# HGRN levels scored in pairs, state updates and scores in fewer runs, and the running maximum spread through DRAM, in a decoder layer on one core

## The chip, the cores and the metric

The kernel runs on one core of one Trainium2 chip. The metric is the device time of one execution in microseconds (us); the median of the runs shown is given. TensorE does the matmuls, VectorE (DVE), ScalarE (ACT) and GpSimd (POOL) the elementwise work, SyncE (SP) starts most DMAs.

## What is computed

One layer on x of 512 tokens by 1024 channels, all in float32:

```python
x = x + 0.5 * rms_norm(swiglu_ffn(rms_norm(x, pre0), ffn1_in, ffn1_out), post0)
x = x + rms_norm(token_mixer(rms_norm(x, pre1)), post1)
x = x + 0.5 * rms_norm(swiglu_ffn(rms_norm(x, pre2), ffn2_in, ffn2_out), post2)
```

The token mixer projects its input by one matrix of 4104 columns and feeds two causal mixers of four heads each. HGRN2 is a gated linear recurrence, S_t = diag(f_t) S_{t-1} + k_t v_t^T and o_t = S_t^T q_t. The mLSTM also keeps a matrix state C, and it scales its scores by exp(a_s - M_t), where M is a running maximum over the tokens, one row per head. The outputs of both are normalised, gated and projected back.

## The kernel before, in words

**Dense work.** Every large product is made of float32r matmuls in three parts, high by high, high by low and low by high (`mm3`, L124-128, and `in_k`, L429-433). Weights come by DMA from SP into a ring (`load`, L183), ACT rounds the high part (L208), DVE takes the low part (L210).

**The mixer stage** (L1388) has two kinds of TensorE work. The column groups of the projection are jobs, written as generators: `job_f` (L746) yields 8 times with 6 matmuls of 256 columns each, `job_t` (L762) yields 32 times with 3 matmuls of 512 columns each. `fill(n)` (L732) takes n such steps from the queue of jobs, and `until(name)` (L741) takes steps until a job is done. Between the fills stand the small float32 matmuls of the mixers, written out by hand in the order in which TensorE does them. A planner puts the instructions of each engine in order ahead of time, by when it expects them to be ready; on the chip each engine keeps that order.

**HGRN.** Inside a chunk of 128 tokens the scores are made by levels of block sizes 64, 32, 16, 8, 4 and 2 (`LEVELS`), for two heads at a time (pass 0 and pass 1). A level (`hgrn_level`, L1038) has four steps: two DVE subtractions and two ACT exponentials (L1050 to L1053); a DVE product (L1055); 32 or 64 recorded small matmuls that use 32 columns of the array (L1068), 640 of them in all; and `put`, which places the scores. `hgrn_levels` (L1073) prepares level n+1, fills 7 steps (pass 0) or 5 (pass 1), and then scores level n. The tag `st` has four buffers, and the levels share them with the convolution and the mLSTM; the two `ke` tiles are taken in turn. `hgrn_states` (L1099) computes the states after chunks 0, 1 and 2 with two fill steps behind each.

**mLSTM.** `gate_rows` (L1150) makes the four rows of -M as a float32r pair `nm` (L1170, L1171). `neg_m` (L1190) spreads a row over the 128 partitions with a matmul by a selector `sel` (L1193), which `masks` builds on POOL (L912 to L922). It is called six times: once per head for the gains e (L1217 to L1221) and once per pair of heads for the decays (L1266 to L1277). The scores (L1231) use 64 rows of the array, the keys are transposed (L1283), and the updates of the state C (L1297) use 64 of its columns, in three runs with two fill steps behind each.

**Gain rows.** The tiles `gpre` and `gpost` hold a norm's gain on all partitions. `gain` (L97, DMA at L99) loads them on SP's queue; `mix_out0` asks for `gpost` and the third norm for `gpre`, both after the mixers.

Of the kernel before, what the change touches and what calls it, by code (L numbers as in the profile page):

```python
# [26 lines left out]
FILL = (7, 5, 2, 2)  # L27
# [40 lines left out]
class Layer:  # L68
    def __init__(self, ctx, tc, aps):
        self.tc, self.nc = tc, tc.nc  # L70
        self.__dict__.update(aps)
        nc = self.nc
        pool = lambda name, **kw: ctx.enter_context(tc.tile_pool(name=name, bufs=1, **kw))
        self.cp, self.wp, self.sp, self.psp = pool("cp"), pool("wp"), pool("sp"), pool("psp", space=PSUM)
        self.uid, self.hold = 0, ()
        self.wt, self.free, self.slot = None, deque(range(WBUF)), {}

        self.ident = self.cp.tile([P, P], F32, name="ident")
        make_identity(nc, self.ident)
# [7 lines left out]
    def nm(self, s):  # L87
# [3 lines left out]
    def ps(self):  # L91
        return self.psp.tile([P, 512], F32, tag="ps", bufs=8, name=self.nm("ps"))

    def col(self, n=1):
        return self.sp.tile([P, n], F32, tag=f"col{n}", bufs={1: 12}.get(n, 4), name=self.nm("col"))

    def gain(self, tag, row):  # L97
        g = self.cp.tile([P, D], F32, tag=tag, bufs=1, name=self.nm(tag))
# [3 lines left out]
    def gain_pe(self, tag, row):  # L102

        nc = self.nc
        g = self.cp.tile([P, D], F32, tag=tag, bufs=1, name=self.nm(tag))
# [58 lines left out]
    def load_due(self, n):  # L164
        lds = self.due.pop(n, ())
        for ld in lds:
            pool = self.wp if ld.ring == "raw" else self.hpool
            self.raw[ld.key] = pool.tile([P, ld.a, ld.b], F32, tag=ld.ring, bufs=ld.depth, name=self.nm(ld.ring))
# [173 lines left out]
    def junk(self):  # L342
        return self.sp.tile([P, 512], F32, tag="junk", bufs=1, name=self.nm("junk"))
# [17 lines left out]
    def pre(self, i, g):  # L361
# [6 lines left out]
        else:  # L368
            xn = self.sp.tile([P, D], F32, tag="xn", bufs=1, name=self.nm("xn"))
# [86 lines left out]
    def open_ffn(self, ctx):  # L456

        hp = self.hpool = ctx.enter_context(self.tc.tile_pool(name=self.nm("hp"), bufs=1))
        self.hf = hp.tile([P, NF, T], F32, name=self.nm("hf"))
        self.xf = [self.hf[:, j : j + 2, :].rearrange("p a (b t) -> p (a b) t", t=HALF) for j in (NF - 4, NF - 2)]  # L460
        sq = [hp.tile([P, 2 * D + PAD], F32R, tag="s", bufs=3, name=self.nm("sq")) for _ in range(3)]
# [203 lines left out]
    def h_tile(self, k2, dst=None):  # L665

        t = dst
        if t is None:
            t = self.place(self.hpool.tile([P, 2 * D + PAD], F32R, tag="s", bufs=3, name=self.nm("hs")), 2)
# [213 lines left out]
    def masks(self, mc, mb):  # L883
# [27 lines left out]
        sel = mb.tile([4, 6, 2, 64], F32, tag="tmp", bufs=1, name="sel")  # L911
        nc.gpsimd.memset(sel, 1.0)  # L912
        self.sel = mc.tile([36, 6, P], F32R, name="selr")
        nc.gpsimd.memset(self.sel.bitcast(I32), 0)
        for n in range(6):
            pat = [[0, 2], [0, 64]] if n < 4 else [[-1, 2], [0, 64]]
            base = -n if n < 4 else -2 * (n - 4)
            nc.gpsimd.affine_select(
                sel[:, n], sel[:, n], pattern=pat, compare_op=ALU.is_equal, fill=0.0, base=base, channel_multiplier=1
            )  # L920
        for r in (0, 32):
            nc.gpsimd.tensor_copy(self.sel[r : r + 4], sel.rearrange("p n a b -> p n (a b)"))  # L922
    def forget_gates(self, mb):
# [4 lines left out]
        for p in range(2):  # L928
            f = (self.sp, mb)[p].tile([P, 2, T], F32, tag=("xn", "tmp")[p], bufs=1, name=self.nm("f"))
# [8 lines left out]
        for p, f in enumerate(fs):  # L938
# [5 lines left out]
            kk = mb.tile([P, 2, T], F32, tag="kk", bufs=2, name=self.nm("kk"))  # L944
# [4 lines left out]
        for p, f in enumerate(fs):  # L949
            G = mb.tile([P, 2, T], F32, tag="G", bufs=2, name=self.nm("G"))  # L950
# [7 lines left out]
    def st(self, name, n=512, dt=F32):  # L958
        return self.sp.tile([P, n], dt, tag="st", bufs=4, name=self.nm(name))

    def hgrn_decays(self, p):
# [14 lines left out]
        d = self.sp.tile([P, 2, T], F32, tag="xn", bufs=1, name=self.nm("ek"))  # L976
# [15 lines left out]
    def hgrn_lowest(self, p):  # L992
# [5 lines left out]
        one = self.sp.tile([P, 2, T], F32, tag="xn", bufs=1, name=self.nm("one"))  # L998
# [74 lines left out]
    def hgrn_levels(self, p, kes, per, then=lambda: None):  # L1073
# [4 lines left out]
        self.fill(per // 2)  # L1078
        next(L[0])
        d = self.hgrn_decays(p)  # L1080
        self.fill(per // 2)
        next(L[1])
        next(L[0])
        self.fill(per)
        for n in range(1, N):
            if n == 2:
                self.hgrn_edges(p, d)
                then()
            if n + 1 < N:
                next(L[n + 1])  # L1090
            next(L[n])
            if n > 1:
                next(L[n - 1])
            self.fill(per)
            next(L[n])
        next(L[N - 1])
        self.spread(p)

    def hgrn_states(self):  # L1099

        nc = self.nc
        for c in range(NT - 1):
            ps = self.ps()
            for h in range(NH):
                nc.tensor.matmul(
                    ps[:, h * P : (h + 1) * P], self.kdt[:, h, c * P : (c + 1) * P], self.vh[:, c, h, :], start=True, stop=True
                )
            if c == 0:
# [7 lines left out]
            self.fill(2)  # L1116
# [33 lines left out]
    def gate_rows(self, mc):  # L1150
# [17 lines left out]
        nm = mc.tile([36, T], F32R, name="nm2")  # L1168
        nc.gpsimd.memset(nm.bitcast(I32), 0)
        nc.vector.tensor_scalar(nm[0:4], M, -1.0, None, op0=ALU.mult)  # L1170
        nc.vector.scalar_tensor_tensor(nm[32:36], M, -1.0, nm[0:4].bitcast(F32), op0=ALU.mult, op1=ALU.subtract)  # L1171
        self.nm2 = nm
# [17 lines left out]
    def neg_m(self, n):  # L1190
        ps = self.ps()
        mm = self.nc.tensor.matmul
        mm(ps, self.sel[:, n, :], self.nm2, start=True, stop=True)  # L1193
        return ps

# [12 lines left out]
    def mlstm_pair(self, p):  # L1208

        nc = self.nc  # L1210
        es = []
        for h in (2 * p, 2 * p + 1):
            nm = self.neg_m(h)
            nm4 = nm.rearrange("p (c t) -> p c t", c=NT)
            e = self.st("e")
            e4 = e.rearrange("p (c t) -> p c t", c=NT)
            nc.vector.tensor_tensor(e4, nm4, self.aT[:, :, h : h + 1].broadcast_to([P, NT, P]), op=ALU.add)  # L1217
            nc.vector.tensor_copy(self.nend[:, h, :].rearrange("p (c o) -> p c o", o=1), nm4[:, :, P - 1 : P])
            nc.vector.tensor_scalar(e, e, 0.0, None, op0=ALU.min)
            nc.scalar.activation(e, e, AF.Exp)  # L1220
            nc.gpsimd.affine_select(  # L1221
                e4, e4, pattern=[[0, NT], [1, P]], compare_op=ALU.is_ge, fill=0.0, base=0, channel_multiplier=-1
            )
            es.append(e)
            yield
        scs = [self.ps(), self.ps()]
        for c in range(NT):
            s = slice(c * P, (c + 1) * P)
            for a in range(2):
                o = slice(64 * a, 64 * a + 64)  # L1230
                nc.tensor.matmul(scs[a][:, s], self.qk[o, 2 + p, s], self.qk[o, p, s], start=True, stop=True)  # L1231
        yield
        for a in range(2):
            nc.vector.scalar_tensor_tensor(self.pT[:, 2 * p + a, :], scs[a], 0.125, es[a], op0=ALU.mult, op1=ALU.mult)
        yield

    def mlstm_scores(self, mc):

        nc = self.nc
        self.nend = mc.tile([P, NH, NT], F32, name="nend")  # L1240
        self.pT = mc.tile([P, NH, T], F32, name="pT")
        H = [self.mlstm_pair(p) for p in range(2)]
        next(H[0])
        next(H[0])
        self.fill(3)
        next(H[1])
        self.fill(3)
        next(H[0])
        next(H[0])
        next(H[1])  # L1250
        self.fill(6)
        next(H[1])
        next(H[1])
        w = mc.tile([P, NT, NH], F32, name="w")
        nc.vector.tensor_tensor(w, self.aT, self.nend.rearrange("p h c -> p c h"), op=ALU.add)
        nc.scalar.activation(w, w, AF.Exp)
        self.qdm = mc.tile([P, 2, 3 * P], F32, name="qdm")
        self.kw = mc.tile([P, 2, 3, P], F32, name="kw")

        self.C = mc.tile([P, 2, 3, 258], F32, name="C")  # L1260
        nc.gpsimd.memset(self.C, 0.0)
        dcs = []
        for p in range(2):
            nm = self.neg_m(4 + p)
            ns = self.st("ns")
            nc.scalar.copy(ns, nm)  # L1266
            n4 = ns.rearrange("p (c t) -> p c t", c=NT)
            d = self.st("dq", 3 * P)
            nc.vector.tensor_tensor(
                d.rearrange("p (c t) -> p c t", c=3), n4[:, 1:, :], n4[:, :3, P - 1 : P].broadcast_to([P, 3, P]), op=ALU.subtract  # L1270
            )
            nc.scalar.activation(d, d, AF.Exp)
            dc = self.col(2)
            nc.vector.tensor_tensor(
                dc.rearrange("p (c o) -> p c o", o=1), n4[:, 1:3, P - 1 : P], n4[:, 0:2, P - 1 : P], op=ALU.subtract
            )
            nc.scalar.activation(dc, dc, AF.Exp)  # L1277
            dcs.append(dc)
            wp = self.col(8)[:, :6]
            nc.vector.tensor_copy(wp.rearrange("p (c a) -> p c a", a=2), w[:, :3, 2 * p : 2 * p + 2])  # L1280
            pt = self.ps()
            for c in range(3):
                nc.tensor.transpose(pt[:, c * P : (c + 1) * P], self.qk[:, 2 + p, c * P : (c + 1) * P], self.ident)  # L1283
            nc.vector.tensor_tensor(
# [6 lines left out]
            self.fill(3)  # L1291
        for c in range(3):
            for p in range(2):
                ps = self.ps()
                for a in range(2):
                    r, v = slice(64 * a, 64 * a + 64), slice(129 * a, 129 * a + 129)
                    nc.tensor.matmul(  # L1297
# [272 lines left out]
```

## Time and profile before

| | before |
|---|---|
| median of 3 runs | 943.44 us (942.9 to 943.52) |
| profiled execution | 943.6 us, of which the span is 941.9 us |
| TensorE (PE) busy | 933.0 us |
| VectorE / ScalarE / GpSimd busy | 701.1 / 470.0 / 291.1 us |
| granted TensorE clock | 0.999 |

The span runs from the first to the last instruction of the profiled execution; 1.7 us of its time lie around it. PE is the row of matmuls, PEld that of the weight loads ahead of them. Matmuls overlap in the records, so what one costs is read from start to start. A row of the timeline gives start, duration, engine, line, operation, tiles, shape and how many records it merges; a float32 matmul leaves two records. A row of a group gives busy time and the mean of one in ns, then the idle time before it.

### The profile page before, as it was taken

What the parts mean: (1) busy time and instruction counts of PE and PEld (TensorE: products, weight loads), DVE (VectorE), ACT (ScalarE), POOL (GpSimd) and SP (SyncE); (2) the same over time, 40 slices, a digit from 0 to 9 for tenths busy, and PEclk for the clock granted to TensorE, in tenths of its full rate; (3) what the DMA queues carried; (4) which work ended last, traced back from release to release, by engine and by line L of the source; (5) the groups of instructions that cost most, each with busy time, mean ns of one, the idle gap of its engine ahead of it and who ended that gap; (6) DMA issues with size and microseconds to landing.
All of it is one profiled execution on the core that took longest, in us unless ns stands there. A gap on an engine that the chain in (4) does not pass through costs nothing.

```text
span 941.9 us, 16851 instructions
## 1 busy us (share of the span) xinstructions
PE 933.0 (99%) x7027; PEld 851.7 (90%) x7027; DVE 701.1 (74%) x788; ACT 470.0 (50%) x641; POOL 291.1 (31%) x234
## 2 busy tenths in 40 slices
PE   9999999999999999999999999999999999999997
PEld 7999999999888889998777888999999999988885
DVE  6798999998545466798746665887999999844543
ACT  7645444445434345987634254753544444533431
POOL 3545555661000037200011301354555655100001
PEclk9999999999999999999999999999999999999999
DMA  9243333425332006331222126204324332332202
GB/s 319 85 135 113 112 110 118 133 90 162 106 104 98 0 23 167 104 91 54 83 69 68 45 76 216 90 26 133 113 90 135 119 106 91 112 106 96 90 0 90
DMA packets 81671, 96.05 MB, mean 102 GB/s; under 512 B 4117, under 2 KB 61497, under 8 KB 81594
## 3 DMA queue, kind: packets, MB, share of 16 engines
q1 hardware_dynamic: 81306, 94.44, 31.3%
q8 instruction: 55, 0.90, 0.4%
q10 hardware_dynamic: 288, 0.52, 0.2%
q14 instruction: 22, 0.18, 0.1%
HBM read 92.85 MB, written 2.10 MB: 101 GB/s over the span
## 4 chain that ended last, share of the span: by engine, by line
PE 92%; DVE 3%; POOL 2%; issue 1%; ACT 1%; DVEq 0%; POOLq 0%; ACTq 0%
PE ps L488 46%; PE ps L126 12%; PE ps L128 12%; PE ps L127 12%; PE ps L433 6%; PE ps L267 1%; PE ps L1068 1%; POOL col L259 1%; POOL col L354 0%; DVE w L216 0%; PE ps L1138 0%; PE ps L115 0%; PE ps L122 0%; DVE y L1330 0%; ACT junk L353 0%
## 5 line engine op out<-in xcount | busy, mean ns | idle before, releaser
L210 DVE TENSOR_TENSOR w<-raw,w 128x1024 fp32r<-128x1024 f32 x214 | 363.0, 1703 | 124.9 <-ACT w L208 124.5
L208 ACT CAST w<-raw 128x1024 fp32r<-128x1024 f32 x214 | 224.0, 1052 | 297.4 <-PE ps L128 96.5
L222 POOL TENSOR_TENSOR raw<-raw,raw 128x1024 f32<-128x1024 f32 x80 | 221.0, 2764 | 171.9 <-DVE w L210 161.4
L488 PE MATMUL ps<-xq,w 128*128 128x256 f32 x2016 | 238.1, 277 | 0.0
L488 PEld LDWEIGHTS ps<-xq,w 128*128 128x128 f32 x2016 | 233.7, 188 | 0.2
L488 PE MATMUL ps<-sq,w 128*128 128x256 f32 x1440 | 171.0, 277 | 0.0
L488 PEld LDWEIGHTS ps<-sq,w 128*128 128x128 f32 x1440 | 167.4, 188 | 0.0
L128 PE MATMUL ps<-w,hs 128*128 128x512 f32 x336 | 131.0, 390 | 0.0
L126 PE MATMUL ps<-w,hs 128*128 128x512 f32 x336 | 130.9, 390 | 0.0
L127 PE MATMUL ps<-w,hs 128*128 128x512 f32 x336 | 130.8, 389 | 0.0
L126 PE MATMUL ps<-w,xq 128*128 128x512 f32 x208 | 84.6, 407 | 0.4 <-DVE y L1371 0.3
L128 PE MATMUL ps<-w,xq 128*128 128x512 f32 x208 | 81.2, 392 | 0.3 <-DVE xq L274 0.3
L127 PE MATMUL ps<-w,xq 128*128 128x512 f32 x208 | 81.3, 392 | 0.0
L128 PEld LDWEIGHTS ps<-w,hs 128*128 128x128 f32 x336 | 63.1, 188 | 13.8 <-DVE hs L672 0.7
L126 PEld LDWEIGHTS ps<-w,hs 128*128 128x128 f32 x336 | 63.1, 188 | 12.9
L127 PEld LDWEIGHTS ps<-w,hs 128*128 128x128 f32 x336 | 63.1, 188 | 12.7
L354 POOL TENSOR_SCALAR col<-col 128x1 f32<-128x1 f32 x24 | 9.6, 398 | 199.3 <-ACT junk L353 199.1
L433 PE MATMUL ps<-xq,w 128*128 128x256 f32 x480 | 55.8, 278 | 0.0
L433 PEld LDWEIGHTS ps<-xq,w 128*128 128x128 f32 x480 | 55.2, 188 | 0.2 <-issue 0.2
L672 DVE TENSOR_TENSOR hs<-hf,hs 128x1024 fp32r<-128x1024 f32 x42 | 51.1, 1217 | 0.0
L126 PEld LDWEIGHTS ps<-w,xq 128*128 128x128 f32 x208 | 39.1, 188 | 10.2 <-issue 1.6
L128 PEld LDWEIGHTS ps<-w,xq 128*128 128x128 f32 x208 | 39.1, 188 | 9.3 <-DVE xq L274 0.8
(235 smaller groups left out, 922.7 us busy)
## 6 DMA issues: line engine op xcount, KB each, us to landing
raw<-in_ffn_w_in_dram SPq DMA_DIRECT2D x88, 512.0 KB, 4.4
raw<-in_ffn_w_out_dram SPq DMA_DIRECT2D x44, 512.0 KB, 3.6
raw<-in_w_mix_in_dram SPq DMA_DIRECT2D x28, 512.0 KB, 3.7
raw<-in_w_mix_out_dram SPq DMA_DIRECT2D x8, 512.0 KB, 3.7
out_dram<-xs SPq DMA_DIRECT2D x8, 256.0 KB, 2.0
xs<-in_x_dram SPq DMA_DIRECT2D x6, 256.0 KB, 6.4
gpost<-in_norm_post_dram SPq DMA_DIRECT2D x3, 512.0 KB
gpre<-in_norm_pre_dram SPq DMA_DIRECT2D x2, 512.0 KB, 4.1
```

The source lines that it names most:

```text
L126: mm(ps, sh, mh, start=start, stop=False, **kw)
L127: mm(ps, sh, ml, start=False, stop=False, **kw)
L128: mm(ps, sl, mh, start=False, stop=stop, **kw)
L208: nc.scalar.copy(hi, raw)
L210: nc.vector.tensor_tensor(lo, raw, hi.bitcast(F32), op=ALU.subtract)
L222: nc.gpsimd.tensor_tensor(o, o, c, op=ALU.add)
L259: nc.gpsimd.tensor_tensor(r, m, self.nhalf[:, :n], op=ALU.pow)
L267: self.nc.tensor.transpose(pt[:, c * P : (c + 1) * P], src[:, k * P : (k + 1) * P], self.ident)
L354: nc.gpsimd.tensor_scalar(m, ss, s2 / D, b, op0=ALU.mult, op1=ALU.add)
L433: mm(ps[:, u0:u1], w[:, a, k, :], self.xop(k, b, u0, u1), start=k + n + m == 0, stop=k == ND - 1 and n == 2, skip_group_check=True,)
L488: self.nc.tensor.matmul(ps[:, c], wb[b][:, k, v], left[d][:, k, :], start=first and a + n + k == 0, stop=n == 2 and k == KH - 1, skip_grou ...
L672: self.nc.vector.tensor_tensor(t[:, 1], src, t[:, 0].bitcast(F32), op=ALU.subtract)
```

## The change

- `hgrn_levels` takes the levels two by two: the small matmuls of levels (1, 2), (3, 4) and (5, 6) stand together, with 15 fill steps ahead of each pair in pass 0 and 12 in pass 1. The next pair is prepared when the last one has been scored.
- `hgrn_states` takes a list: chunks 0 and 1 stand together, and chunk 2 stands ahead of the updates of C. Those are one run; C has 129 columns instead of 258 and its DVE updates take all 128 partitions at once.
- `neg_m`, its selector and its six matmuls go. The rows -M are written to DRAM and read back on all 128 partitions, by three DMAs on POOL's queue, into the tiles `gpre` and `gpost`.
- The gains of all four heads come first; then, for each pair of heads, the decays, the scores and the transposes stand together with 8 fill steps behind them.
- HGRN's values are made two chunks at a time.

The diff, cut to its core (`nm` is renamed `name` everywhere):

```diff
-FILL = (7, 5, 2, 2)
+FILL = (15, 12, 2, 2)
...
+        self.dp = pool("dp", space=bass.MemoryType.DRAM)
...
         next(L[0])
-        self.fill(per // 2)
+        self.fill(3)
         next(L[0])
         d = self.hgrn_decays(p)
-        self.fill(per // 2)
-        next(L[1])
+        self.fill(3)
+        both = lambda n: [next(L[m]) for m in (n, n + 1)]
+        both(1)
         next(L[0])
-        self.fill(per)
-        for n in range(1, N):
-            if n == 2:
+        for n in range(1, N, 2):
+            both(n)
+            if n > 1:
+                both(n - 2)
+            self.fill(per)
+            both(n)
+            if n == 1:
                 self.hgrn_edges(p, d)
                 then()
-            if n + 1 < N:
-                next(L[n + 1])
-            next(L[n])
-            if n > 1:
-                next(L[n - 1])
-            self.fill(per)
-            next(L[n])
-        next(L[N - 1])
+            if n + 2 < N:
+                both(n + 2)
+        both(N - 2)
         self.spread(p)
...
-    def hgrn_states(self):
+    def hgrn_states(self, chunks):
...
-            self.fill(2)
...
-        nm = mc.tile([36, T], F32R, name="nm2")
...
+        nm = mc.tile([4, T], F32, name="nm2")
+        nc.vector.tensor_scalar(nm, M, -1.0, None, op0=ALU.mult)
+        rows = self.dp.tile([4, T], F32, name="mrows")
+        nc.gpsimd.dma_start(rows, nm)
+        self.nm = []
+        for p, tag in enumerate(("gpre", "gpost")):
+            t = self.cp.tile([P, D], F32, tag=tag, bufs=1, name=self.name(tag)).rearrange("p (a t) -> p a t", a=2)
+            nc.gpsimd.dma_start(t, rows[2 * p : 2 * p + 2].rearrange("(o a) t -> o a t", o=1).broadcast_to([P, 2, T]))
+            self.nm += [t[:, 0], t[:, 1]]
...
-    def neg_m(self, n):
-        ps = self.ps()
-        mm = self.nc.tensor.matmul
-        mm(ps, self.sel[:, n, :], self.nm2, start=True, stop=True)
-        return ps
...
+    def mlstm_gains(self, h):
...
+        nc.vector.tensor_tensor(
+            e4, self.nm[h].rearrange("p (c t) -> p c t", c=NT), self.aT[:, :, h : h + 1].broadcast_to([P, NT, P]), op=ALU.add
+        )
+        nc.vector.tensor_scalar(e, e, 0.0, None, op0=ALU.min)
+        nc.scalar.activation(e, e, AF.Exp)
+        nc.gpsimd.affine_select(
+            e4, e4, pattern=[[0, NT], [1, P]], compare_op=ALU.is_ge, fill=0.0, base=0, channel_multiplier=-1
+        )
+        return e
...
+        es = [self.mlstm_gains(h) for h in range(NH)]
+        self.fill(3)
         dcs = []
         for p in range(2):
...
+            for a in range(2):
+                r = slice(64 * a, 64 * a + 64)
+                n4 = self.nm[2 * p + a][r].rearrange("p (c t) -> p c t", c=NT)
+                nc.vector.tensor_tensor(
+                    d[r].rearrange("p (c t) -> p c t", c=3), n4[:, 1:, :], n4[:, :3, P - 1 : P].broadcast_to([64, 3, P]), op=ALU.subtract
+                )
...
+            self.fill(8)
+        self.hgrn_states((2,))
+        banks = [self.ps(), self.ps()]
+        for p in range(2):
+            for c in range(3):
                 for a in range(2):
                     r = slice(64 * a, 64 * a + 64)
...
+                    nc.tensor.matmul(
+                        banks[p][r, 129 * c : 129 * c + 129], self.kw[:, p, c, r], self.vm[:, c, 2 * p + a, :],
+                        start=True, stop=True, skip_group_check=True,
+                    )
...
+        self.fill(4)
...
-                self.hgrn_states()
+                self.hgrn_states((0, 1))
+                self.fill(6)
                 self.mlstm_scores(mc)
...
-                self.chunks(self.hgrn_values, FILL[3])
+                for pair in ((0, 1), (2, 3)):
+                    G = [self.hgrn_values(c) for c in pair]
+                    for _ in range(2):
+                        for g in G:
+                            next(g)
+                        self.fill(2)
+                    self.fill(2)
+                    for g in G:
+                        next(g)
```

More of the change, by code (lines that the diff above doesn't have):

```diff
@@ L456, in open_ffn @@
     def open_ffn(self, ctx):
-        hp = self.hpool = ctx.enter_context(self.tc.tile_pool(name=self.nm("hp"), bufs=1))
-        self.hf = hp.tile([P, NF, T], F32, name=self.nm("hf"))
+        hp = self.hpool = ctx.enter_context(self.tc.tile_pool(name=self.name("hp"), bufs=1))
+        self.hf = hp.tile([P, NF, T], F32, name=self.name("hf"))
         self.xf = [self.hf[:, j : j + 2, :].rearrange("p a (b t) -> p (a b) t", t=HALF) for j in (NF - 4, NF - 2)]
-        sq = [hp.tile([P, 2 * D + PAD], F32R, tag="s", bufs=3, name=self.nm("sq")) for _ in range(3)]
+        sq = [hp.tile([P, 2 * D + PAD], F32R, tag="s", bufs=3, name=self.name("sq")) for _ in range(3)]
         self.sq = [self.place(t, KH, True) for t in sq]
@@ L668, in h_tile @@
         if t is None:
-            t = self.place(self.hpool.tile([P, 2 * D + PAD], F32R, tag="s", bufs=3, name=self.nm("hs")), 2)
+            t = self.place(self.hpool.tile([P, 2 * D + PAD], F32R, tag="s", bufs=3, name=self.name("hs")), 2)
         src = self.hf[:, 2 * k2 : 2 * k2 + 2, :]
@@ L910, in masks @@
             nc.gpsimd.tensor_copy(self.eye[r], square[r, r])
[L911 to L922, printed above, removed]
     def forget_gates(self, mb):
@@ L997, in hgrn_lowest @@
         by2 = lambda t: flat(t).rearrange("p (b two) -> p b two", two=2)
-        one = self.sp.tile([P, 2, T], F32, tag="xn", bufs=1, name=self.nm("one"))
+        one = self.sp.tile([P, 2, T], F32, tag="xn", bufs=1, name=self.name("one"))
         near = self.st("near")
@@ L1107, in hgrn_states @@
                 )
+            banks.append(ps)
+        for c, ps in zip(chunks, banks):
             if c == 0:
@@ L1206, in conv @@
             nc.vector.scalar_tensor_tensor(y[:, s:], x[:, : T - s], tap(j), y[:, s:], op0=ALU.mult, op1=ALU.add)
-    def mlstm_pair(self, p):
+    def mlstm_gains(self, h):
         nc = self.nc
[L1211 to L1235, printed above, removed]
@@ L1237, in mlstm_scores @@
+        return e
     def mlstm_scores(self, mc):
         nc = self.nc
-        self.nend = mc.tile([P, NH, NT], F32, name="nend")
-        self.pT = mc.tile([P, NH, T], F32, name="pT")
[L1242 to L1254, printed above, removed]
@@ L1255, in mlstm_scores @@
-        nc.vector.tensor_tensor(w, self.aT, self.nend.rearrange("p h c -> p c h"), op=ALU.add)
-        nc.scalar.activation(w, w, AF.Exp)
+        nend = mc.tile([P, NH, NT], F32, name="nend")
+        for h in range(NH):
+            nc.vector.tensor_copy(
+                nend[:, h, :].rearrange("p (c o) -> p c o", o=1), self.nm[h].rearrange("p (c t) -> p c t", c=NT)[:, :, P - 1 : P]
+            )
+        self.pT = mc.tile([P, NH, T], F32, name="pT")
         self.qdm = mc.tile([P, 2, 3 * P], F32, name="qdm")
@@ L1258, in mlstm_scores @@
         self.kw = mc.tile([P, 2, 3, P], F32, name="kw")
-        self.C = mc.tile([P, 2, 3, 258], F32, name="C")
-        nc.gpsimd.memset(self.C, 0.0)
+        self.C = mc.tile([P, 2, 3, 129], F32, name="C")
+        w = mc.tile([P, NT, NH], F32, name="w")
+        nc.vector.tensor_tensor(w, self.aT, nend.rearrange("p h c -> p c h"), op=ALU.add)
+        nc.scalar.activation(w, w, AF.Exp)
+        es = [self.mlstm_gains(h) for h in range(NH)]
+        self.fill(3)
         dcs = []
         for p in range(2):
[L1264 to L1271, printed above, removed]
+            d = mc.tile([P, 3 * P], F32, tag="dq", bufs=2, name=self.name("dq"))
+            dc = self.col(2)
+            for a in range(2):
[4 more added lines that the diff above has]
+                )
+                nc.vector.tensor_tensor(
+                    dc[r].rearrange("p (c o) -> p c o", o=1), n4[:, 1:3, P - 1 : P], n4[:, 0:2, P - 1 : P], op=ALU.subtract
+                )
@@ L1281, in mlstm_scores @@
+            for c in range(NT):
+                s = slice(c * P, (c + 1) * P)
+                for a in range(2):
+                    o = slice(64 * a, 64 * a + 64)
+                    nc.tensor.matmul(scs[a][:, s], self.qk[o, 2 + p, s], self.qk[o, p, s], start=True, stop=True)
             pt = self.ps()
@@ L1283, in mlstm_scores @@
                 nc.tensor.transpose(pt[:, c * P : (c + 1) * P], self.qk[:, 2 + p, c * P : (c + 1) * P], self.ident)
+            for a in range(2):
+                h = 2 * p + a
+                nc.vector.scalar_tensor_tensor(self.pT[:, h, :], scs[a], 0.125, es[h], op0=ALU.mult, op1=ALU.mult)
+            wp = self.col(8)[:, :6]
+            nc.vector.tensor_copy(wp.rearrange("p (c a) -> p c a", a=2), w[:, :3, 2 * p : 2 * p + 2])
             nc.vector.tensor_tensor(
@@ L1290, in mlstm_scores @@
             nc.vector.scalar_tensor_tensor(self.qdm[:, p, :], self.qk[:, p, P:], 0.125, d, op0=ALU.mult, op1=ALU.mult)
[L1291 to L1297, printed above, removed]
-                        ps[r, v], self.kw[:, p, c, r], self.vm[:, c, 2 * p + a, :], start=True, stop=True, skip_group_check=True
-                    )
+            self.fill(8)
[3 more added lines that the diff above has]
+            for c in range(3):
                 for a in range(2):
                     r = slice(64 * a, 64 * a + 64)
-                    v = slice(129 * a, 129 * a + 129)
-                    if c == 0:
-                        nc.vector.tensor_copy(self.C[r, p, 0, v], ps[r, v])
-                    else:
-                        nc.vector.scalar_tensor_tensor(
-                            self.C[r, p, c, v], self.C[r, p, c - 1, v], dcs[p][r, c - 1 : c], ps[r, v], op0=ALU.mult, op1=ALU.add
-                        )
-            self.fill(2)
+                    nc.tensor.matmul(
+                        banks[p][r, 129 * c : 129 * c + 129], self.kw[:, p, c, r], self.vm[:, c, 2 * p + a, :],
+                        start=True, stop=True, skip_group_check=True,
+                    )
+        for p in range(2):
+            for c in range(3):
+                ps = banks[p][:, 129 * c : 129 * c + 129]
+                if c == 0:
+                    nc.vector.tensor_copy(self.C[:, p, 0, :], ps)
+                else:
+                    nc.vector.scalar_tensor_tensor(
+                        self.C[:, p, c, :], self.C[:, p, c - 1, :], dcs[p][:, c - 1 : c], ps, op0=ALU.mult, op1=ALU.add
+                    )
+        self.fill(4)
     def hgrn_values(self, c):
@@ L1343, in mlstm_values @@
                         banks[a][:, 129 * p : 129 * p + 129], self.qdm[r, p, (c - 1) * P : c * P],
-                        self.C[r, p, c - 1, 129 * a : 129 * a + 129], start=p == 0, stop=False, skip_group_check=True,
+                        self.C[r, p, c - 1, :], start=p == 0, stop=False, skip_group_check=True,
                     )
```

46 lines of the change are left out of this document (20 added, 26 removed).

## Prediction

> **What bounds the kernel now.** I read the busy shares and the chain first, then what TensorE waited for, then the mixer stage.
>
> ```profile
> span 941.9 us, 16851 instructions
> PE 933.0 (99%) x7027; PEld 851.7 (90%) x7027; DVE 701.1 (74%) x788; ACT 470.0 (50%) x641; POOL 291.1 (31%) x234
> PE 92%; DVE 3%; POOL 2%; issue 1%; ACT 1%; DVEq 0%; POOLq 0%; ACTq 0%
> ```
>
> ```profile
> PE ps L122 <- POOL ident masks.py:199: 1.5, 1, 1.5
> PE ps L126 <- DVE y L1371: 0.3, 1, 0.3
> ```
>
> TensorE is busy for 933.0 of 941.9 us, and its longest wait inside the mixers is 0.3 us. So TensorE time that goes from its queue shortens the kernel one for one, and work taken from other engines is worth nothing by itself. The other engines matter only as a condition: what they prepare must be ready when TensorE comes to it. In the first part of the mixer stage that is close:
>
> ```profile
> 388.00:449.00 61.00, 61.00 (x729) 55.42 (x727) 51.99 (x71) 50.97 (x67) 4.42 (x5) 1.00 0.27 81
> ```
>
> In these 61 us (pass 0 of the levels) TensorE is busy throughout, DVE for 51.99 (85%) and ACT for 50.97 (84%).
>
> **The price of a run of small matmuls.** First the dense pace, then a level of 64 records (two starts and the neighbours), then eight records of a state update.
>
> ```profile
> 454.70 0.39 PE L128 MATMUL ps<-w,xq 128*128 128x512 f32 x1
> ...
> 458.10 0.39 PE L128 MATMUL ps<-w,xq 128*128 128x512 f32 x1
> ...
> 465.46 0.39 PE L127 MATMUL ps<-w,xq 128*128 128x512 f32 x1
> ...
> 468.43 0.39 PE L128 MATMUL ps<-w,xq 128*128 128x512 f32 x1
> 468.75 0.74 PE L1068 MATMUL ps<-qe,ke 128*32 128x16 f32 x64
> ...
> 469.76 0.40 PE L127 MATMUL ps<-w,xq 128*128 128x512 f32 x1
> ```
>
> ```profile
> 483.88 0.40 PE L128 MATMUL ps<-w,xq 128*128 128x512 f32 x1
> 484.12 1.05 PE L1105 MATMUL ps<-vh,kdt 128*128 128x128 f32 x8
> ...
> 485.24 0.39 PE L127 MATMUL ps<-w,xq 128*128 128x512 f32 x1
> ```
>
> ```profile
> L1068 PE MATMUL ps<-qe,ke 128*32 128x16 f32 x512 | 5.9, 185 | 0.0
> L1105 PE MATMUL ps<-vh,kdt 128*128 128x128 f32 x24 | 3.3, 279 | 0.0
> ```
>
> From 454.70 to 458.10 are 15 dense matmuls: 0.2267 us each. From the dense matmul ahead of the level (468.43) to the second one behind it (469.76) are 1.33 us; less two dense ones, 0.88 are the level's. Its matmuls themselves: eight such runs are busy 5.9 us, 0.74 each; less the last one's 0.185, the starts spread over 0.55 us, 0.0088 a record, 0.56 for 64. So 0.88 - 0.56 = **0.32 us belongs to entering and leaving the run**, not to its work. Behind a run the dense pace settles: 465.46 to 468.43 holds 13 matmuls in 2.97 us, 0.02 over the pace. For the state update on the full array: 1.36 - 0.45 = 0.91, its records at (1.05 - 0.28)/7 = 0.11 each make 0.88, and only 0.03 is left. So a run costs extra where it uses part of the array's columns or rows, not because it is float32.
>
> [...]
>
> **The change part by part.**
>
> *Levels in pairs.* Twelve L1068 runs become six, with the same matmuls; levels 1 and 2 of both passes, on 64 and 32 columns of output, use the same part of the array as the others. 6 x (0.32 + 0.02) = 2.0 us.
>
> *The six spreads.* The whole stretch, first and last of its 47 dense matmuls, and its second score run:
>
> ```profile
> 488.44 0.40 PE L128 MATMUL ps<-w,xq 128*128 128x512 f32 x1
> ...
> 499.72 0.39 PE L128 MATMUL ps<-w,xq 128*128 128x512 f32 x1
> 500.04 1.16 PE L1231 MATMUL ps<-qk 64*128 64x128 f32 x16
> 500.95 0.48 PE L1193 MATMUL ps<-nm,selr 36*128 36x512 f32 x1
> 501.36 0.55 PE L1283 MATMUL ps<-ident,qk 128*128 128x128 f32 x3
> ...
> 501.98 0.40 PE L127 MATMUL ps<-w,xq 128*128 128x512 f32 x1
> ...
> 504.94 0.40 PE L127 MATMUL ps<-w,xq 128*128 128x512 f32 x1
> ```
>
> 488.44 to 504.94 is 16.50 us; less 47 x 0.2267 = 10.65, 5.85 are the small runs'. After the change two runs are left, scores and transposes. Such a run took 2.26 - 0.45 = 1.81 with a spread of 0.41 in it: 1.40 without, if no switch from 64 rows to the full array shows in its place, 1.81 if all of it does. I take 1.45, near the low end, since a switch stood on both sides of the spread already. 5.85 - 2 x 1.45 = 2.95 us (bounds 2.2 and 3.05).
>
> *State updates.*
>
> ```profile
> 506.54 0.39 PE L128 MATMUL ps<-w,xq 128*128 128x512 f32 x1
> ...
> 512.14 0.39 PE L127 MATMUL ps<-w,xq 128*128 128x512 f32 x1
> ```
>
> ```profile
> L1297 PE MATMUL ps<-vm,kw 128*64 128x129 f32 x24 | 2.0, 286 | 0.0
> ```
>
> Three runs of C cost 5.60 - 14 x 0.2267 = 2.43 us, the third state update 0.91. One run of both: 0.88 + 24 records at (0.667 - 0.286)/7 = 0.054, so 1.31, + one boundary, 2.43/3 - 8 x 0.054 = 0.37; 2.56 in all. Saved 0.78. Three full-array merges: 0.08.
>
> *Fill steps.* The same jobs are done, and by the code the 132 steps ahead of the states and the 64 behind them stay between the same ends. Nothing.
>
> *DVE, ACT, POOL.* C's updates go from twelve to six, two copies on ACT, a memset and the selector on POOL go, four halves of the decays replace two whole ones. None is on the path.
>
> *The rows.*
>
> ```profile
> 448.77 0.68 DVE L1171 SCALAR_TENSOR_TENSOR nm<-rowt,nm 4x512 fp32r<-4x512 f32 x1
> ```
>
> ```profile
> 489.31 0.69 DVE L1217 TENSOR_TENSOR e<-ps,aT 128x512 f32<-128x512 f32 x1 [0.69 <-PE ps L1193]
> ```
>
> ```profile
> gpre<-in_norm_pre_dram SPq DMA_DIRECT2D x2, 512.0 KB, 4.1
> rows<-in_conv_w_dram SPq DMA_DIRECT2D x1, 8.0 KB, 8.5
> ```
>
> ```profile
> L1261 POOL MEMSET C<- 128x1548 f32 x1 | 1.4, 1393 | 91.8 <-ACT sT L1036 91.8
> ```
>
> The rows exist at about 449, the first gain wants them at about 489, or some 3 us sooner when the levels are shorter. The write (8 KB landed in 8.5 us), then two loads (4.1 each): 17 us against 37. No DMA on POOL's queue is in this trace; at twice these prices it is still hidden. What queues behind the waiting DMAs on POOL is nothing until the masks of the gains: POOL idled 91.8 us there. The price is nothing; if the cover of 37 us were gone, each us late is a us of the kernel.
>
> **Sum.** 2.0 + 2.95 + 0.78 + 0.08 = 5.8 us. 943.6 - 5.8 = 937.8; the median stands 0.16 below the profiled execution, so **937.6**. One bound: the 0.3 us wait above, on the banks of job "mo", cost 0.5 with its restart; that job now starts a fill step later, and the wait may go (937.1). The other: 0.75 less from the spreads (938.4).
>
> **Rivals.**
>
> *Pairs not ready, once.* A pair's preparation can start only when the pair before is scored, for the buffers of `st` and `ke`.
>
> ```profile
> L1050 DVE TENSOR_TENSOR qe<-G 128x512 f32<-128x512 f32 x8 | 5.5, 686 | 0.1
> ```
>
> ```profile
> L1052 ACT ACTIVATE qe<-qe 128x512 f32<-128x512 f32 x8 | 5.0, 629 | 1.5 <-DVE qe L1050 1.5
> L1429 ACT ACTIVATE qk<-qk 128x2048 f32<-128x2048 f32 x1 | 1.9, 1915 | 0.0
> L1429 ACT ACT_TABLE_LOAD x1 | 1.3, 1283 | 0.3 <-DVE qk L1206 0.3
> ```
>
> ```profile
> 399.64 12.28 PE L433 MATMUL ps<-xq,w 128*128 128x256 f32 x102
> ```
>
> The chain is four subtractions, the last exponential and two products: 4 x 0.69 + 0.63 + 2 x 0.69 = 4.8 us. Its cover is 15 steps at 12.28/17 = 0.72, 10.8 us. For it: DVE at 85% has 9.2 us of work in that time, so even with everything else first the chain ends in time. Against it: the Silu of q and k with a table load on each side (4.5 us) may be put ahead of the exponentials of levels 5 and 6; 9.2 + 4.5 is 2.9 late. Once: 940.5.
>
> *Pairs not ready, everywhere: slower.* The same wait ahead of the second and third pair of pass 0. It decides from 2.9 us at each, the gain then being gone; with 4.5 at each the time is 937.6 + 9 = 946.6.
>
> *A gain load holds SP's queue.* The loads of `gpost` and `gpre` must now wait for the last reader of the rows, and weight loads stand behind them.
>
> ```profile
> SPq L99 <- DVE ps L390: 21.1, 2, 20.9
> ```
>
> ```profile
> 483.99 10.89 SPq L183 DMA_DIRECT2D raw<-in_w_mix_in_dram  x2
> ```
>
> ```profile
> 516.28 1.04 ACT L208 CAST w<-raw 128x1024 fp32r<-128x1024 f32 x1
> ```
>
> Such a load held the queue for 20.9 us elsewhere. The second of the two loads here is issued at 494.5 and first read at 516.3, so some 18 us of hold cost nothing; a hold of 40 would cost up to 22: 960.
>
> *The rows come late.* It decides from 20 us beyond the 17 worked out, from DMAs on POOL; at 27 beyond, 937.6 + 7 = 945. [...]
>
> *Not what it says.* The planner puts fill steps between the levels of a pair: 939.6 without the 2.0.
>
> **Chances.** Forecast 0.68 (936.5 to 939), once late 0.12, not paired 0.05, late everywhere 0.07, SP held 0.05, rows late 0.03. The measurement tells about 0.2% (1.9 us) from no change. Faster: 0.68 + 0.05 + 0.10 of the once-late, 0.83. Same: the rest of the once-late and 0.01 of late rows, 0.03. Slower: what is left, 0.14. The range that holds the first three is 936.0 to 942.0.
>
> **What would show it.** Six L1068 runs instead of twelve; no L1193; one run of L1105 and L1297; span near 936 with TensorE's idle time in the mixers still under 1 us. Waits of L1068 on `ke` or `qe` mean the second or third rival; a wait of dense matmuls on a `w` that came late by DMA means SP; a wait of L1217's successor on DMA means the rows. If the span falls by much less with no wait, the price of a boundary, 0.32, is what I had wrong.

## The result, and the profile after

The changed kernel takes 939.62 us (median of 11 executions, 938.8 to 942.92), the kernel before 943.44 beside it: ratio 0.9972, 95% interval 0.9959 to 0.9984. That is 3.8 us by the medians, where 5.8 were forecast. The 11 times fall in two groups, six from 938.8 to 939.62 and five from 941.53 to 942.92; the profile shown is of an execution of the second group (942.87 us).

Its page: span, busy shares, and the engines' shares of the chain that ended last.

```profile
span 941.2 us, 16822 instructions
PE 930.8 (99%) x7021; PEld 854.0 (91%) x7021; DVE 698.1 (74%) x785; ACT 469.3 (50%) x639; POOL 286.7 (30%) x225
PE 91%; ACT 3%; DVE 3%; issue 1%; DMA 1%; POOL 0%; DVEq 0%; POOLq 0%; ACTq 0%
```

TensorE has six matmuls less, the spreads, and is still busy 99%. But the chain now has ACT at 3% instead of 1%, and a DMA. What TensorE waited for longest in the whole span (line, releaser, us in total, times, longest); the first matmuls of the kernel have the other one:

```profile
PE ps L1177 <- ACT sT L1016: 2.0, 1, 2.0
PE ps L123 <- POOL ident masks.py:199: 1.6, 1, 1.6
```

The wait ahead of the values (0.3 on job mo's banks) is gone, and a new one of 2.0 us is there: the eight small transposes that bring the gate rows to tokens (`by_tokens`, L1177 and L1178) waited for ScalarE's copy of level 1's scores (`put`, L1016). The timeline of TensorE at that place, in pass 1:

```profile
457.70 1.58 PE L1058 MATMUL ps<-qe,ke 128*32 128x64 f32 x64
459.22 0.87 PE L979 MATMUL ps<-ident,ek 128*128 128x128 f32 x6
462.10 0.23 PE L1177 MATMUL ps<-ident,z 4*128 4x4 f32 x1 [2.00 <-ACT sT L1016]
...
463.59 0.63 PE L128 MATMUL ps<-w,xq 128*128 128x512 f32 x1
464.02 0.63 PE L129 MATMUL ps<-w,xq 128*128 128x512 f32 x1
...
469.08 0.40 PE L129 MATMUL ps<-w,xq 128*128 128x512 f32 x1
```

The first pair's scores, the edges, then nothing until 462.10. Behind the wait the dense matmuls start 0.43 us apart (463.59, 464.02) instead of 0.227, until 469.08: TensorE ran at half pace for 7.0 us.

Why was the copy late? VectorE ahead of it, then ScalarE, then the three DMAs of the rows on POOL's queue, and the same three with their KB and the us from issue to landing:

```profile
456.60 0.33 DVE L1240 TENSOR_TENSOR col<-gpre 64x2 f32<-64x2 f32 x2 [1.42 <-DMA gpre<-mrows]
459.54 0.33 DVE L1240 TENSOR_TENSOR col<-gpost 64x2 f32<-64x2 f32 x2 [2.61 <-DMA gpost<-mrows]
459.90 2.40 DVE L211 TENSOR_TENSOR w<-raw,w 128x1024 fp32r<-128x1024 f32 x2
```

```profile
456.96 0.20 ACT L1244 ACTIVATE col<-col 128x2 f32<-128x2 f32 x1 [2.02 <-DVE col L1240]
...
459.90 0.20 ACT L1244 ACTIVATE col<-col 128x2 f32<-128x2 f32 x1 [1.31 <-DVE col L1240]
460.01 1.03 ACT L209 CAST w<-raw 128x1024 fp32r<-128x1024 f32 x1
460.95 0.63 ACT L1043 ACTIVATE ke<-el 128x512 f32<-128x512 f32 x1
461.48 0.82 ACT L1016 COPY sT<-ps 64x512 f32<-64x512 f32 x2
```

```profile
448.40 0.77 POOL L1163 DMA_DIRECT2D mrows<-nm  x1 [75.09 <-DVE nm L1161]
451.72 0.58 POOL L1167 DMA_DIRECT2D gpre<-mrows  x1 [2.56 <-DMA mrows<-nm]
452.29 0.53 POOL L1167 DMA_DIRECT2D gpost<-mrows  x1
```

```profile
gpre<-mrows POOLq DMA_DIRECT2D x1, 512.0 KB, 4.9
gpost<-mrows POOLq DMA_DIRECT2D x1, 512.0 KB, 7.2
...
mrows<-nm POOLq DMA_DIRECT2D x1, 8.0 KB, 3.0
```

The readers of the rows that come first are not the gains but four subtractions of two columns (L1240, the decays of the state C). In the code they stand behind both passes of levels and the first state updates, yet they need nothing but the rows and a small buffer that is free, and the planner put them among pass 1's levels. On the chip VectorE came to them before the rows had landed and stood there 1.42 + 2.61 = 4.0 us; ScalarE stood 2.02 + 1.31 = 3.3 us for the exponentials behind them (L1244). Casts that needed nothing of the rows (L209, L211) stood behind these in their queues. On VectorE the rows show it: the first of the two low parts (L211) reads the cast that ScalarE had done by 458.58 (457.54 + 1.04), and starts at 459.90, when the second pair of subtractions is through.

And why did the transposes want that copy? By the code they need a ninth bank. Of the eight, four are a projection job's sums, two the pair's scores, two the edges; before the change only one level's scores were open there.

### The profile page after: what moved, and what is told of

The parts are those of the page before. It is cut to its first block, busy times and chain, and to the rows that moved or that the text cites. A ratio compares the mean times of both kernels' runs of the same rounds, so it can differ in the third digit from the quotient of the medians.

```text
span 941.2 us, 16822 instructions
## 1 busy us (share of the span) xinstructions
PE 930.8 (99%) x7021; PEld 854.0 (91%) x7021; DVE 698.1 (74%) x785; ACT 469.3 (50%) x639; POOL 286.7 (30%) x225
## 4 chain that ended last, share of the span: by engine, by line
PE 91%; ACT 3%; DVE 3%; issue 1%; DMA 1%; POOL 0%; DVEq 0%; POOLq 0%; ACTq 0%
PE ps L489 46%; PE ps L127 12%; PE ps L129 12%; PE ps L128 12%; PE ps L434 3%; PE ps L268 1%; PE ps L444 1%; DVE qk L1196 1%; DMA gpost<-mrows 1%; DVE w L211 1%; PE ps L1327 0%; ACT w L209 0%; PE ps L1295 0%; PE ps L116 0%; PE ps L123 0%
## 5 line engine op out<-in xcount | busy, mean ns | idle before, releaser
L211 DVE TENSOR_TENSOR w<-raw,w 128x1024 fp32r<-128x1024 f32 x214 | 362.5, 1701 | 132.2 <-ACT w L209 131.9
L209 ACT CAST w<-raw 128x1024 fp32r<-128x1024 f32 x214 | 224.1, 1053 | 314.1 <-PE ps L129 112.5
L129 PE MATMUL ps<-w,hs 128*128 128x512 f32 x336 | 131.0, 390 | 0.0
L127 PE MATMUL ps<-w,hs 128*128 128x512 f32 x336 | 130.9, 390 | 0.0
L127 PE MATMUL ps<-w,xq 128*128 128x512 f32 x208 | 84.5, 406 | 0.1
L129 PE MATMUL ps<-w,xq 128*128 128x512 f32 x208 | 81.9, 396 | 0.0
L129 PEld LDWEIGHTS ps<-w,hs 128*128 128x128 f32 x336 | 63.1, 188 | 13.8 <-DVE hs L673 0.7
L127 PEld LDWEIGHTS ps<-w,hs 128*128 128x128 f32 x336 | 63.1, 188 | 12.8
L129 PEld LDWEIGHTS ps<-w,xq 128*128 128x128 f32 x208 | 39.7, 191 | 9.1 <-DVE xq L275 0.3
L127 PEld LDWEIGHTS ps<-w,xq 128*128 128x128 f32 x208 | 39.8, 191 | 8.9 <-ACT xq L274 0.7
```

What stands on the lines that cost most here:

```text
L127: mm(ps, sh, mh, start=start, stop=False, **kw)
L129: mm(ps, sl, mh, start=False, stop=stop, **kw)
L209: nc.scalar.copy(hi, raw)
L211: nc.vector.tensor_tensor(lo, raw, hi.bitcast(F32), op=ALU.subtract)
```

## The experiments

**Theory A:** the missing time is this wait, and it takes two things together: the ninth bank, and the copy that frees a bank being late because two engines stand at the rows' DMA. **Rival B:** the bank alone does it. **Rival R:** standing engines delay TensorE wherever it goes next. **Rival S:** the terms of the sum were too large, whatever waits show. Times below are medians, each with the kernel before on the same chip.

### The transposes later (tok_late)

```
                 self.hgrn_edges(p, d)
-                then()
...
             self.fill(per)
+            if n == 3:
+                then()
             both(n)
```

> The changed kernel with the eight small transposes of the gate rows moved from right behind the edges to behind the second pair's fill steps, where three banks are free. Theory A (the missing 2.0 us are one wait: the transposes need a ninth bank, which only level 1's copy frees, and that copy is late on ScalarE because VectorE and ScalarE stand at the rows' DMA): the wait goes although VectorE still stands about 4.0 us at the DMA, no dense matmul runs at half pace, 939.62 - 2.0 = 937.6 and all executions within 1 us of each other. Rival R (VectorE standing at the DMA is what delays TensorE, whatever stands next in its queue): a wait of about 2 us comes at another place, 939.6. Rival S (the terms of the sum are smaller than worked out): 939.6 with TensorE's longest wait in the mixers under 0.5 us.

937.91 us (937.37 to 938.58) against 943.52: ratio 0.9941, 0.9929 to 0.9953. VectorE's own waits, 449 to 463 us, are still there:

```profile
DVE col L1241 <- DMA gpost<-mrows: 2.8, 1, 2.8
DVE col L1241 <- DMA gpre<-mrows: 1.2, 1, 1.2
```

TensorE waited nowhere in the mixers. Rivals R and S fall.

### The subtractions later (dc_late, both_late, dc_late_kept, both_late_kept)

```
-            dc = self.col(2)
+            dc = mc.tile([P, 2], F32, tag="dc", bufs=2, name=self.name("dc"))
```

> The changed kernel with the four two-column subtractions that stood at the rows' DMA given a tile of the later pool, so that they come behind the levels on VectorE's queue; the transposes stay where they are. Theory A: VectorE's 4.0 us and ScalarE's 3.3 us of standing go, level 1's copy follows the pair's scores at once, and of the 2.0 us at the transposes 0 to 0.8 stay: 937.6 to 938.4. Rival B (the ninth bank alone does it, the rows have no part): 2.0 us stay at the transposes, 939.6. Rival S: 939.6 without a wait.

> Both edits. Theory A: no wait over 0.3 us in the mixers and 937.4 (the sum of the prediction, 5.8, plus 0.3 for the wait before job mo that no longer shows, less 0.25 for the score runs). Rival S: 938.6 or more with no wait, the price of a boundary being under 0.32.

947.46 (ratio 1.0043, 1.0029 to 1.0056) and 948.21 us (1.0042, 1.003 to 1.0055): neither what A nor what a rival said, and no wait in the mixers. The loss was elsewhere. Groups of matmuls of dc_late by what they read (count, us busy, mean ns):

```profile
L489 PE MATMUL ps<-xq,w 128*128 128x256 f32 x2016 | 237.4, 276 | 0.0
L489 PE MATMUL ps<-sq,w 128*128 128x256 f32 x1440 | 176.3, 280 | 0.0
L127 PE MATMUL ps<-w,hs 128*128 128x512 f32 x336 | 132.7, 395 | 0.0
```

The same groups of dc_late_kept, where `self.col(2)` is still called ahead of the new line and its result left unused:

```profile
L489 PE MATMUL ps<-xq,w 128*128 128x256 f32 x2016 | 238.1, 277 | 0.0
L489 PE MATMUL ps<-sq,w 128*128 128x256 f32 x1440 | 171.0, 277 | 0.0
...
L127 PE MATMUL ps<-w,hs 128*128 128x512 f32 x336 | 130.9, 390 | 0.0
```

> As dc_late, with the small pool's two-column buffers still reserved, though unused. In dc_late they had fallen away, which moved the tiles of the pool behind them, the feed-forward layers' among them, by 4 x 8 = 32 bytes in each partition; the queues' orders are the same. If that shift is what cost dc_late 8 us (its matmuls on sq took 280 ns instead of 277 and those on hs 395 instead of 390, those on xq the same), this one shows 277 and 390 again and the time theory A gave for dc_late, 937.6 to 938.4. If it was the later subtractions themselves: 947 again.

> As both_late, with the same buffers still reserved. Theory A: 937.2 to 937.9, no wait over 0.3 us in the mixers; the same as tok_late within 0.5, since there VectorE's standing cost TensorE nothing. Rival S: 938.6 or more.

Both take 937.16 us (936.99 to 938.19 and 936.7 to 937.62) against 943.56: ratios 0.9934 (0.9922 to 0.9946) and 0.9933 (0.9921 to 0.9945). The 32 bytes cost 947.46 - 937.16 = 10.3 us, nearly all in feed-forward matmuls that the edit doesn't touch: the busy time grew by 5.3 on `sq` and by about 1.8 in each of the three groups on `hs` (L127 to L129). With the layout kept, theory A holds from its other side. TensorE of dc_late_kept, the transposes still right behind the edges:

```profile
458.27 1.58 PE L1058 MATMUL ps<-qe,ke 128*32 128x64 f32 x64
459.79 0.87 PE L979 MATMUL ps<-ident,ek 128*128 128x128 f32 x6
460.59 0.22 PE L1177 MATMUL ps<-ident,z 4*128 4x4 f32 x1
```

Same place, same banks, no wait: the copy followed the scores at once. Rival B falls. These two beat the changed kernel by 2.5 us and the kernel before by 6.4.

### The pairs alone, and all but the pairs

pairs_alone is the kernel before with the new `hgrn_levels` and `FILL`; no_pairs is the changed kernel with the old ones.

> The kernel before with the levels in pairs and nothing else of the change: rows by matmul, states and C in their old runs. Sum of the prediction for the pairs: 943.44 - 2.0 = 941.4. Theory A: no DMA stands ahead of level 1's copy, so the ninth bank costs 0 to 0.8: 941.4 to 942.2. Rival B: 2.0 at the transposes, 943.4. Rival S: no wait and 942.4 or more, the six boundaries being worth 1.0 or less.

> The changed kernel with the levels as before, in twelve runs, and all else changed. Theory A: the transposes find eight banks as before, so no wait over 0.5 us although VectorE stands at the rows' DMA; 937.9 (the changed kernel with its transposes late) + 1.85 (what the pairs alone gave) = 939.8, which is also about what the whole change came to with its wait. Rival R: a wait of 2 us for a level's operands behind the standing VectorE: 941.8. Rival S (the spreads and states are worth less than 3.7): 941 or more without a wait.

pairs_alone: 941.67 us (941.07 to 942.31) against 943.52, ratio 0.9981 (0.9972 to 0.999); no wait at the transposes though the ninth bank is there. no_pairs: 939.32 us (938.68 to 939.8) against 943.56, 0.9955 (0.9943 to 0.9967); no wait in the mixers though the rows come by DMA. Its transposes, and ScalarE's copy of level 1:

```profile
460.68 0.22 PE L1177 MATMUL ps<-ident,z 4*128 4x4 f32 x1
```

```profile
461.26 0.58 ACT L1016 COPY sT<-ps 64x512 f32<-64x512 f32 x1
```

The copy comes after the transposes have begun and doesn't hold them. VectorE stood at the rows for only 0.30 + 1.30 = 1.6 us here, so for a full stand without the ninth bank tok_late is the better witness. Neither half has the wait; only the two together. The pairs are worth 943.52 - 941.67 = 1.85 on the old kernel and 939.32 - 937.16 = 2.16 on the changed one without its wait, and all the rest 943.56 - 939.32 = 4.24.

### The wait and the half pace (after_again, wait1, wait2, hop)

> The changed kernel itself, on the chip of the others. Its times fell in two groups, 938.8 to 939.6 and 941.5 to 942.9, and the one profile shown is of the second: behind the 2.0 us wait 12 or 13 dense matmuls ran 0.426 us apart instead of 0.227. If the wait always comes and the half pace only sometimes, times of both groups come again, and a profile of the first group shows the wait of 1.3 to 2.0 us and no half pace behind it. If the first group is without the wait, the wait depends on when the rows land.

The changed kernel again: 940.45 us (938.67 to 944.81), 0.9971 (0.996 to 0.9982); of 12 times six are below 940 and six from 941.1 up. This time the profile is of the first group (939.8 us):

```profile
462.33 0.22 PE L1177 MATMUL ps<-ident,z 4*128 4x4 f32 x1 [2.27 <-ACT sT L1016]
...
463.50 0.40 PE L129 MATMUL ps<-w,xq 128*128 128x512 f32 x1
463.73 0.40 PE L127 MATMUL ps<-w,xq 128*128 128x512 f32 x1
```

A longer wait than in the first profile, and full pace behind it. Windows of 449 to 482 us (length, then busy time of PE, PEld, DVE, ACT and POOL, the granted clock, DMA share, GB/s), the first profile and then this one:

```profile
449.00:482.00 33.00, 31.00 (x310) 25.29 (x309) 19.69 (x35) 18.32 (x31) 3.04 (x5) 0.90 0.37 112
```

```profile
449.00:482.00 33.00, 30.73 (x431) 25.21 (x431) 19.79 (x37) 19.69 (x34) 3.00 (x5) 1.00 0.42 127
```

Granted clock 0.90 against 1.00. The clocks of whole executions show the same split in both sets of runs: 0.999 in all twelve executions below 940 us, 0.994 to 0.997 in all eleven above 941. So the half pace comes in about half the executions, and is the distance between the groups. The wait stands in both profiles; that it comes every time is read from the times alone, since the fastest of the 23 executions, 938.67 us, is slower than every one of tok_late, dc_late_kept and both_late_kept (938.58 at most).

To vary the wait's length, the next two add needless copies of level 1's scores on ScalarE ahead of the one that frees the bank, in dc_late_kept: one in wait1 (shown), two in wait2.

```
+            if p == 1 and n == 1:
+                for _ in range(1):
+                    self.nc.scalar.copy(self.junk()[:64], sc[:64])
             for b in range(64 // c):
```

> As dc_late_kept (no wait at the transposes, 937.16), with one needless copy of 64x512 on ScalarE ahead of level 1's copy in pass 1. The bank comes free some 0.6 us later, so TensorE waits 0.3 to 0.6 us there. If a wait costs its own length: 937.6. If any wait at this place brings the half pace in some executions: two groups of times, some 2 us apart.

> The same with two such copies; on ScalarE's queue level 2's copy, both copies of the edges and two exponentials then come between them, so the bank comes free some 4.1 us after the scores and TensorE waits about 3.3 us. If a wait costs its own length: 940.5, all executions within 1 us. If the half pace behind a wait depends on its length (none at 0.5, half the executions at 2.0 to 2.3): nearly all executions carry it, 942.5 to 944.5. If it comes by chance at any wait: two groups again.

937.25 (937.16 to 937.3) and 937.57 us (937.34 to 939.8), ratios 0.9935 (0.9921 to 0.9948) and 0.9943 (0.993 to 0.9955), and no wait at this place: the planner saw the copies coming, and let TensorE do two dense matmuls ahead of the transposes in both. So they say nothing of the pace; they fit the reading that this place stalls where the delay is one that the planner's order doesn't allow for, as the DMA's was. The last run therefore lengthens the DMA:

```
-        nc.gpsimd.dma_start(rows, nm)
+        first = self.dp.tile([4, T], F32, name="mfirst")
+        nc.gpsimd.dma_start(first, nm)
+        nc.gpsimd.dma_start(rows, first)
```

> The changed kernel with the rows written to DRAM twice, one DMA behind the other, before they are spread. By the changed kernel's own trace the write landed 2.6 us after POOL began to wait for it, so the rows land 2 to 4 us later, VectorE stands that much longer, and the wait at the transposes grows from 2.0-2.3 to 4 to 6 us. If a wait costs its own length and the half pace comes by chance, as in the changed kernel: two groups of times, near 942.5 and 945. If the half pace depends on the wait's length: all executions carry it, 944.5 to 946, in one group. If the rows' landing is not what sets the wait: 939.4 and 941.5, as without the second write.

942.33 us (939.59 to 944.84), ratio 0.9988 (0.9979 to 0.9996). One of its VectorE rows, and TensorE (profile of the slowest execution, 944.84 us):

```profile
460.27 0.32 DVE L1242 TENSOR_TENSOR col<-gpre 64x2 f32<-64x2 f32 x2 [5.48 <-DMA gpre<-mrows]
```

```profile
464.30 0.26 PE L1179 MATMUL ps<-ident,z 4*128 4x4 f32 x1 [4.60 <-ACT sT L1016]
...
466.26 0.63 PE L129 MATMUL ps<-w,xq 128*128 128x512 f32 x1
466.69 0.63 PE L127 MATMUL ps<-w,xq 128*128 128x512 f32 x1
...
471.27 0.40 PE L129 MATMUL ps<-w,xq 128*128 128x512 f32 x1
```

VectorE stands 5.48 us, and the wait of TensorE is 4.60. After that stand VectorE does one low part of 1.22 us, which the planner put between the two pairs of subtractions, and comes to the second pair at 461.76 instead of 459.54, 2.2 later; the transposes, at 464.30 instead of 462.10, start 2.2 later too. So the landing of the rows sets the wait. The times are neither of the patterns expected, two groups or one, but a spread. Since a wait 2.3 us longer alone would put an execution near 941.6, a time can't tell whether the half pace was there. By the clock nine of the 12 executions (0.994 to 0.997) have it as the second group above has, and three (0.998 and 0.999) do not show it; against 11 of 23 that is too few to say that a longer wait brings it more often.

## Why the prediction was wrong, step by step

**The boundaries held.** Six L1058 runs, no spread, one run of state update and C, as said. Their prices from the profile after, each from the dense matmul ahead of the run to the third behind it, less three at 0.2267:

```profile
473.89 0.39 PE L129 MATMUL ps<-w,xq 128*128 128x512 f32 x1
474.20 1.32 PE L1058 MATMUL ps<-qe,ke 128*32 128x16 f32 x128
...
476.04 0.40 PE L129 MATMUL ps<-w,xq 128*128 128x512 f32 x1
```

```profile
492.97 0.39 PE L129 MATMUL ps<-w,xq 128*128 128x512 f32 x1
493.28 1.16 PE L1251 MATMUL ps<-qk 64*128 64x128 f32 x16
...
495.23 0.40 PE L129 MATMUL ps<-w,xq 128*128 128x512 f32 x1
...
507.05 0.40 PE L129 MATMUL ps<-w,xq 128*128 128x512 f32 x1
507.28 1.06 PE L1096 MATMUL ps<-vh,kdt 128*128 128x128 f32 x8
508.27 1.54 PE L1274 MATMUL ps<-vm,kw 128*64 128x129 f32 x24
...
510.31 0.40 PE L129 MATMUL ps<-w,xq 128*128 128x512 f32 x1
```

- *Pairs, 2.0:* a pair of 128 records costs 476.04 - 473.89 - 3 x 0.2267 = 1.47, where two levels cost 2 x 0.88. The runs measured 1.85 and 2.16 for all six. Right.
- *Spreads, 2.95:* a score run costs 2.26 - 0.68 = 1.58, not 1.45, which by the prediction's own reading means that a part of the switch from 64 rows to the full array is back; no run separates it. 5.85 - 2 x 1.58 = 2.69. The forecast was a little too large; the measured value is inside its bounds.
- *States and C, 0.78:* the one run costs 3.26 - 0.68 = 2.58, forecast 2.56. Right.
- *The wait ahead of job mo:* named as a bound, worth 0.5 with its restart; it is gone.

Together 2.0 + 2.69 + 0.76 + 0.08 + 0.5 = 6.0, of which the last two are the prediction's estimates, which no run measured alone: three merges between full-array runs at the 0.03 or so read from the state update of before, and the wait with its restart. The kernel without its new wait gained 6.4, so the sum was right, if anything small, and 937.6 lies between dc_late_kept (937.16) and tok_late (937.91).

**"DVE, ACT, POOL ... None is on the path" and "the first gain wants them at about 489" failed.** The cover of the rows was counted to the reader that I knew from the trace of before. But a DMA's cover ends at the first instruction that reads it in its engine's order, and the planner moved the readers forward: the first gain from 489.3 to 477.2, and the first subtraction of two columns, which stood at 502.97 before, ahead of all the others. VectorE reached that subtraction at 455.2 (456.60 less the 1.42 that it stood there), 6.8 us behind the write's issue at 448.40; the cover was 6.8 and not 37. The latency itself was smaller than worked out: from 448.40 to 459.5 (452.29 + 7.2), 11 us for 17. So the price was called nothing by a wrong end of the cover, not by a wrong latency. I asked what queues behind the waiting DMAs on POOL, and not what queues behind the waiting reader on VectorE.

**The banks were never counted.** Two levels scored together hold two banks until their copies, and that made the copy a condition for TensorE's next work. I gave pairs a condition on what comes into them (`ke`, `st`), none on what must leave.

**The rivals.** No L1058 run waited for its operands: both "pairs not ready" are out. "Rows come late" was the nearest: late rows did cost, but from 7 us on and not from 37, through a bank and not through the gains. "A gain load holds SP's queue" did happen, too briefly to cost anything: the two loads waited on that queue for the last reader of the rows.

```profile
SPq L100 <- DVE dq L1237: 5.4, 2, 4.4
```

That is 5.4 us where the prediction had worked out that some 18 are free, and no matmul waited for weights behind it.

The issues on POOL took 0.77, 0.58 and 0.53 us. What sets the landings of the two DMAs of 512 KB stays open: they took 4.9 and 7.2 us here, 4.0 and 4.8 in hop, where VectorE stood idle for most of that time, but 4.2 and 5.3 in no_pairs, where it worked for most of it.

**The balance:** 6.4 gained, 2.0 to 2.3 given back, by the times in every execution (about 939.3, the first group), and some 3 more in the executions with the half pace.

## What to carry to other kernels

When a value starts to come by DMA, look for its smallest and most movable reader, not its main one: here VectorE's queue stood at it for 4.0 us and ScalarE's for 3.3, and what came behind was late. When work is merged, count what it holds open at once (here banks) at the next point that allocates one. And behind any edit that adds or drops a buffer, compare a matmul far from the edit: if its mean has moved (here from 277 to 280 ns and from 390 to 395, for 32 bytes), look at the layout first.

## What the runs showed of the hardware

**The clock.** A wait of 2.00 us was followed by 7.0 us of half pace (462.10 to 469.08), one of 4.60 by 7.0 as well (464.30 to 471.27), one of 2.27 by none. The price of the half pace can be read between the two profiles of the changed kernel: the next pair starts at 474.20 and at 471.34, 2.86 apart, and the first had 0.27 less of wait: about 3.1 us, more than the wait. The wait of 2.00 us stood behind 2.4 us of small matmuls (457.70 to 460.1), and that of 2.27 behind the same 2.4 (457.67 to 460.06). What brings the half pace behind one wait and not behind another was not shown.

**Placement.** Moving tiles by 32 bytes (by the code; the traces show no addresses) took the matmuls that read `sq` from 277 to 280 ns and those that read `hs` from 390 to 395 ns, while the largest group, on `xq`, whose tiles stayed, kept 276 to 277: 10.3 us of 937. A small group that reads `xq` and `sq` (288 matmuls) went the other way, from 282 to 280. What it is in the placement that counts wasn't tried.
